# Down-projections of a decoder trunk's third part regrouped into four pairs with a ninth tile apart, and two units per feed-forward block put on ScalarE and VectorE in written order

## The chip, the core and the metric

The kernel runs on one core of a Trainium2 chip. The metric is the device time of one execution in microseconds (us); before the change it is 1767.26 us, the median of three runs (1767.1 to 1767.7). Five engines are named as in the profile: PE (TensorE, matrix products; PEld is its weight load), DVE (VectorE), ACT (ScalarE), POOL (GpSimd) and SP (SyncE, which issues the loads).

## The reference

Two layers, each a feed-forward block (SwiGLU), a token mixer (causal convolution beside differential attention), and a second feed-forward block; all data are float32. The change touches the four feed-forward blocks and one sum of squares.

```python
D_MODEL, SEQ, DEPTH, D_FF = 1024, 512, 2, 2816

def rms_norm(x, g):
    return x * lax.rsqrt(jnp.mean(x * x, axis=-1, keepdims=True) + EPS) * g

def swiglu(h, w_gate, w_up, w_down):
    return (jax.nn.silu(h @ w_gate) * (h @ w_up)) @ w_down

for l in range(DEPTH):
    x = x + 0.5 * swiglu(rms_norm(x, ffn1_norm[l]), ffn1_w_gate[l], ffn1_w_up[l], ffn1_w_down[l])
    x = x + mixer(rms_norm(x, mix_norm[l]))
    x = x + 0.5 * swiglu(rms_norm(x, ffn2_norm[l]), ffn2_w_gate[l], ffn2_w_up[l], ffn2_w_down[l])
```

## The kernel before

**Number format.** PE multiplies in a reduced float32 form. Every operand is therefore split: ACT writes its rounded copy ("hi"), DVE subtracts that from the operand and writes the rest ("lo"), and each product is three matmuls: hi by hi, hi by lo, lo by hi (`product`, L380 to L389). A matmul here has 128 rows of weights and 128 columns; what varies is the width of what streams past, 256 or 512.

**Three parts of a feed-forward block.** The 22 tiles of 128 hidden channels are worked in three parts of 5, 8 and 9 (`PARTS`, L45). The first is computed plainly. The other two are cut into units with Strassen's scheme (seven half-size products in place of eight): a `GateUp` unit (L464) computes gate and up of one hidden tile in 7 products of 4 steps, 84 matmuls of width 256; a `Down` unit (L511, four to a part, q = 0 to 3) computes two output tiles from the part's hidden tiles. A Down unit takes hidden tiles in pairs: p pairs cost 7 products of p steps, 21 p matmuls of width 256; every hidden tile outside the pairs ("plain") costs 6 matmuls of width 512. `PARTS` gives four pairs of eight tiles to the second part, and three pairs and three plain tiles of nine to the third.

**Names in a unit** (`Unit.body`, L399 to L451): a product is named by its weights, such as "u2u1", "u2", "g1", "g2", "all", "g1u2u1"; the seventh, "g1u1", is run inside the next unit (`rest`). Results lie in PSUM halves a, d (first bank) and b, c (second bank). ACT copies some out into `keep` (L405, L422, L442), DVE adds them up (`close`, `rest`).

**Weights.** While a unit runs, the next one's weights are made ready: SP loads them into a ring of five buffers `wraw`, POOL forms the weight sums (L360 to L363), ACT and DVE split four tiles A, B, C (width 1024) and D (width 512) into `whi` and `wlo` (L370, L374; rings of four, and of two for D). In the third part the ninth tile's weights are appended to C and D.

**Hidden tiles.** `Gated` (L633) keeps each hidden tile's hi and lo (`hh`, `hl`), and for a pair the sums "t2", "t3" and "t4" (`hs`, made by `combine`, L691). The unit that follows the last gate of a part and stands before its first Down ("spare" unit) is in the second part the first gate of the third; the third part has none, its ninth gate runs ahead of the second part's Downs.

**Order.** PE's products stand in written order (L389 pins the first matmul of each). Everything else is ordered by a scheduler, on each engine, from the written program. Finished rows of x are normalised for the next block by `Prep.tile` (L229: hi, lo and the square, which POOL adds to `ssum`, L244).

Of the kernel before, what the change touches and what calls it, by code (L numbers as in the profile page):

```python
# [18 lines left out]
P = 128  # L19
# [25 lines left out]
PARTS = ((0, 5, 0), (5, 8, 4), (13, 9, 3))  # L45
# [3 lines left out]
SPACE = 312  # L49
# [21 lines left out]
def trunk(ctx: ExitStack, tc: tile.TileContext, xt, par, lamv, relb, onehot,  # L71
# [110 lines left out]
    ones = const.tile([P, P], F32, tag="ones", name="ones")  # L182
    G.memset(ones, 1.0)
# [37 lines left out]
    class Prep:  # L221
# [16 lines left out]
        def squares(self, k, pin=False):  # L238
            sq = self.s if k == 0 else tmp.tile([P, SEQ], F32, tag="sq", name="sq")
            square = S.activation(sq, x[:, k, :], AF.Square)  # L240
            if pin:
                tc.keep_in_program_order(square)
            if k > 0:
                (V if pin else G).tensor_tensor(self.s, self.s, sq, op=ALU.add)  # L244
# [105 lines left out]
    class Unit:  # L350
# [49 lines left out]
        def body(self, nxt, prev, prev2):  # L400
# [8 lines left out]
            if not self.sums_last:  # L409
                self.go(self.d, "u2", "t4", first=True)  # L410
            self.early()
            if nxt and self.early_free:
                nxt.hi("B")
            if self.sums_last:
                self.go(self.a, "g1", "b11", first=True)
            if prev:
                prev.rest()
            if self.sums_last:
                self.go(self.d, "u2", "t4")
            else:  # L420
                self.go(self.a, "g1", "b11")
# [3 lines left out]
            if nxt and self.early_free:  # L425
                nxt.lo("B")
# [13 lines left out]
            self.go(self.c, "all", "b22")  # L440
            self.go(self.a, "g1u2u1", "t2")
            pinned(S.activation(self.keep[:, 2], self.a, AF.Copy))  # L442
            self.close()
            if nxt:
                nxt.lo("C")
                if not self.early_free:
                    nxt.hi("B")
                    nxt.lo("B")

        early_free, soon, sums_last = True, False, False  # L450
# [13 lines left out]
    class GateUp(Unit):  # L464
        steps = KT // 2

        def __init__(self, fp, halves, g, u, n, gated):
            super().__init__(fp)
            self.halves, self.src, self.n, self.gated = halves, (g, u), n, gated
            self.soon = n == 2 * gated.pairs - 1 and n + 1 == gated.many  # L470
# [33 lines left out]
        def finish(self, n):  # L504
            if self.soon and n == 0:
                self.gated.combine(self.n, self.banks[0], self.banks[1][:, :HS])
            self.gated.add(self.n, self.banks[0], n)

        def combine(self):
            self.gated.combine(self.n, self.banks[0])  # L510

    class Down(Unit):
        def __init__(self, fp, dn, m0, many, pairs, q, h, after, early_free, last):
# [3 lines left out]
            self.early_free = early_free  # L517
            self.sums_last = not q and 2 * pairs == many

        def load(self):  # L520
            A, B = 2 * self.q, 2 * self.q + 1
            whole, over, J = min(self.many, 8), max(self.many - 8, 0), self.steps * P
# [16 lines left out]
            at = {"D": J, "C": 2 * J}  # L539
            raw = {"D": d, "C": more}  # L540
            where = ("D", "D") if J + 2 * over * P <= 512 else ("D", "C")
            self.ninth = []
            for n, m in enumerate((A, B)):
                k = where[n]
                self.ninth.append((k, at[k] // P))
                pull(raw[k], at[k], m, whole, self.many)
                at[k] += over * P
# [9 lines left out]
            cols = {"A": whole * P, "B": whole * P, **at}  # L557
            self.raw = {k: t[:, : cols[k]] for k, t in (("A", u), ("B", g), ("C", more), ("D", d))}

# [7 lines left out]

        def plain(self, ps, n, first=False):
            if 2 * self.steps == self.many:
                return  # L570
            w = [
                self.w("BA"[n], k) if k < 8 else self.w(*self.ninth[n])
                for k in range(2 * self.steps, self.many)
            ]
            self.product(ps, zip(w, (self.h.hh[k] for k in range(2 * self.steps, self.many))), first)

        def spare(self):
            if 2 * self.steps < self.many:
                self.ps = bank(("tp", "y")[self.q % 2], "ps_d")
                self.plain(self.ps, 1, first=True)  # L580

        def early(self):
            if self.early_free and not self.last:
                self.spare()

        def middle(self):
            if self.early_free and not self.last:
                self.plain(self.banks[1], 0)

# [5 lines left out]
        def close(self):  # L595
            A, B = 2 * self.q, 2 * self.q + 1
            two, keep = by_two(self.banks[1]), self.keep
            late = not self.early_free or self.last
            rest = 2 * self.steps < self.many
            if self.last:  # L600
                self.spare()
            elif late:
                self.plain(self.banks[1], 0)
            pinned(V.tensor_tensor(two, two, keep[:, 0::2], op=ALU.add))
            if self.last:
                self.plain(self.banks[1], 0)
            else:
                self.into(A, two, 0.5)
                self.after(A)
            if late and not self.last:  # L610
                self.spare()
            if rest:
                pinned(V.tensor_tensor(by_two(self.ps), by_two(self.ps), keep[:, 1::2], op=ALU.subtract))
                self.into(B, by_two(self.ps), 0.5)
            if self.last:
                self.into(A, two, 0.5)
                self.after(A)

        def rest(self):
            self.go(self.a, "g1u1", "t3")  # L620
            B = 2 * self.q + 1
            if 2 * self.steps < self.many:
# [6 lines left out]

    class Gated:  # L630

        def __init__(self, fp, pairs, many):
            self.fp, self.pairs, self.many = fp, pairs, many  # L633
            self.hold = ("hh7", "hl7") if many > 8 else ("hh8", "hl8")
            self.hh, self.sums, self.held, self.slots = {}, [], {}, []

        def part(self):

            if not self.slots:
# [3 lines left out]
                tags += [(tmp, "ssum", 1), (tmp, "sq", None), (tmp, "sq", None)]  # L643
                self.slots += [
                    lambda pool=pool, tag=tag, bufs=bufs: pool.tile(
                        [P, SEQ], F32R, tag=tag, name="hs", **({"bufs": bufs} if bufs else {}))
                    for pool, tag, bufs in tags
                ]
            return self.slots.pop(0)()

# [10 lines left out]
        def add(self, n, us, step):  # L661
            a, b = slice(0, HS), slice(HS, SEQ)
            first = self.paired(n) and n % 2 == 0
            if step == 0:
                if first:
                    self.held[n] = self.fp.tile([P, SEQ], F32, tag=self.hold[n // 2 % 2], name="hold")
# [12 lines left out]
        def part_hi(self, n, us):  # L679
            hi = self.fp.tile([P, SEQ], F32R, tag=f"hh{n}", name="hh")  # L680
            lo = self.fp.tile([P, SEQ], F32R, tag=f"hl{n}", name="hl")
# [7 lines left out]
        def combine(self, n, us, last=None):  # L689
# [9 lines left out]
            pinned(S.activation(four[:, a], last, AF.Copy))  # L699
            pinned(S.activation(hi, t, AF.Copy))  # L700
            pinned(V.tensor_tensor(four[:, b], last, f32(four[:, a]), op=ALU.subtract))
            pinned(V.tensor_tensor(lo, t, f32(hi), op=ALU.subtract))
            self.sums.append((hi, lo, four))
# [9 lines left out]
    def ffn(pr, gu, dn, after, turn, lead=None, aside=None):  # L713
        with tc.tile_pool(name="ffn", bufs=1) as fp:
# [50 lines left out]
            for m0, many, pairs in PARTS[1:]:  # L765
                h = Gated(fp, pairs, many)
                gates = [
                    GateUp(fp, halves, gu[m0 + n, 0], gu[m0 + n, 1], n, h)
                    for n in (*range(8, many), *range(min(many, 8)))
                ]  # L770
                end = m0 + many == FT
                units += gates[:1] + downs + gates[1:]
                downs = [
                    Down(fp, dn, m0, many, pairs, q, h, after if end else lambda m: None, q > 0 or not end,
                         end and q == KT // 2 - 1)
# [7 lines left out]
            for k in "ABDC":  # L783
                units[0].hi(k, False)
                units[0].lo(k, False)
            for n, unit in enumerate(units):
# [470 lines left out]
```

## Time and profile before

| | value |
|---|---|
| median of three runs | 1767.26 us |
| the profiled execution's own time | 1767.6 us |
| its span (first to last instruction) | 1765.8 us |
| granted TensorE clock, whole span | 1.0 |
| busy: PE / DVE / ACT / POOL | 99% / 79% / 56% / 49% |

The profile describes one execution. A row of the timeline gives start, duration, engine, line, operation, and in square brackets what ended a wait. A row of the groups gives the number of instructions, their total busy time, the mean of one in ns, and the engine's idle time just before them with its releaser. PE's durations overlap: a matmul of width 256 is shown with 0.28 us although the next one starts sooner, so the pace is read from start to start.

### The profile page before, as it was taken

Reading aid. Unit: us, or ns where it says so; the run is one execution under the profiler, and the core shown is the slowest. Engines: PE = TensorE matmul, PEld = TensorE weight load, DVE = VectorE, ACT = ScalarE, POOL = GpSimd, SP = SyncE. Lnnn points to the kernel's source line nnn. Section 1 sums busy time; section 2 is a strip of 40 time slices with the busy share of each in tenths; the row PEclk is TensorE's granted clock in tenths of the full one; section 3 lists DMA queues with packets and bytes.
Section 4 is the critical chain, followed back from the end, with each engine's and each line's share of the span. In section 5 each row is a group of like instructions: output and inputs, shape, how many; then the busy total and the mean of one; then the engine's idle time right before and its main releaser. Section 6 shows DMA issues by size and latency. Waiting matters only on the chain.

```text
span 1765.8 us, 30565 instructions
## 1 busy us (share of the span) xinstructions
PE 1756.3 (99%) x11869; PEld 1620.8 (92%) x11869; DVE 1394.2 (79%) x2021; ACT 989.1 (56%) x1591; POOL 869.5 (49%) x665
## 2 busy tenths in 40 slices
PE   9999999999999999999999999999999999999999
PEld 7899999988788899999988999999887888999998
DVE  6978878868857868878778788777788588788785
ACT  6456565545845456556534665565558354565653
POOL 3165655369753146555303565543687432556551
PEclk9999999999999999999999999999999999999999
DMA  6233333333122233333332333334230232333332
GB/s 226 92 117 100 106 108 105 127 104 99 33 84 84 84 96 108 109 102 117 106 108 72 108 99 105 108 98 154 72 119 25 72 108 72 107 98 108 108 106 75
DMA packets 82930, 177.89 MB, mean 101 GB/s; under 512 B 8951, under 2 KB 30726, under 8 KB 82784
## 3 DMA queue, kind: packets, MB, share of 16 engines
q1 hardware_dynamic: 81184, 174.10, 31.2%
q8 instruction: 93, 1.52, 0.4%
q0 software_dynamic: 1312, 1.67, 0.3%
q14 instruction: 53, 0.43, 0.1%
q10 hardware_dynamic: 288, 0.16, 0.0%
HBM read 173.79 MB, written 3.42 MB: 100 GB/s over the span
## 4 chain that ended last, share of the span: by engine, by line
PE 97%; DVE 2%; DMA 0%; issue 0%; SPq 0%; ACT 0%; DVEq 0%
PE ps_pair L387 57%; PE ps_pair L147 5%; PE ps_pair L146 5%; PE ps_pair L143 5%; PE ps_d L147 2%; PE ps_d L146 2%; PE ps_d L143 2%; PE ps_sc L1028 2%; PE ps_d L387 2%; PE ps_pair L904 2%; PE ps_pair L905 2%; PE ps_pair L906 2%; PE ps_out L146 1%; PE ps_out L147 1%; PE ps_out L143 1%; PE ps_o L1058 1%
## 5 line engine op out<-in xcount | busy, mean ns | idle before, releaser
L374 DVE TENSOR_TENSOR wlo<-wraw,whi 128x1024 fp32r<-128x1024 f32 (+2 forms) x400 | 505.6, 1264 | 167.3 <-ACT whi L370 166.6
L370 ACT ACTIVATE whi<-wraw 128x1024 fp32r<-128x1024 f32 (+2 forms) x400 | 379.2, 949 | 329.4 <-PE ps_pair L387 184.5
L360 POOL TENSOR_TENSOR wraw<-wraw 128x512 f32<-128x512 f32 (+1 forms) x100 | 113.1, 1131 | 605.9 <-DVE wlo L374 393.9
L387 PE MATMUL ps_pair<-acth,wlo 128*128 128x256 f32 x1088 | 307.9, 283 | 0.0
L387 PE MATMUL ps_pair<-actl,whi 128*128 128x256 f32 x1088 | 307.9, 283 | 0.0
L387 PE MATMUL ps_pair<-acth,whi 128*128 128x256 f32 x1088 | 307.9, 283 | 0.0
L387 PE MATMUL ps_pair<-th,whi 128*128 128x256 f32 x816 | 230.9, 283 | 0.0
L387 PE MATMUL ps_pair<-tl,whi 128*128 128x256 f32 x816 | 230.9, 283 | 0.0
L387 PE MATMUL ps_pair<-th,wlo 128*128 128x256 f32 x816 | 230.9, 283 | 0.0
L387 PEld LDWEIGHTS ps_pair<-actl,whi 128*128 128x128 f32 x1088 | 208.9, 192 | 0.2
L387 PEld LDWEIGHTS ps_pair<-acth,whi 128*128 128x128 f32 x1088 | 208.9, 192 | 0.2
L106 ACT ACTIVATE whi<-wraw 128x1024 fp32r<-128x1024 f32 (+3 forms) x124 | 123.2, 1002 | 153.0 <-PE ps_pair L146 85.7
L387 PEld LDWEIGHTS ps_pair<-acth,wlo 128*128 128x128 f32 x1088 | 208.9, 192 | 0.0
L362 POOL TENSOR_TENSOR wraw<-wraw 128x512 f32<-128x512 f32 (+1 forms) x100 | 176.5, 1765 | 7.8
L146 PE MATMUL ps_pair<-actl,whi 128*128 128x512 f32 x448 | 174.7, 391 | 0.3
L143 PE MATMUL ps_pair<-acth,whi 128*128 128x512 f32 x448 | 173.7, 392 | 0.7 <-ACT whi L106 0.6
L147 PE MATMUL ps_pair<-acth,wlo 128*128 128x512 f32 x448 | 173.8, 390 | 0.0
L387 PEld LDWEIGHTS ps_pair<-th,whi 128*128 128x128 f32 x816 | 156.7, 192 | 0.0
L387 PEld LDWEIGHTS ps_pair<-tl,whi 128*128 128x128 f32 x816 | 156.7, 192 | 0.0
L387 PEld LDWEIGHTS ps_pair<-th,wlo 128*128 128x128 f32 x816 | 156.7, 192 | 0.0
L363 POOL TENSOR_TENSOR wraw<-wraw 128x512 f32<-128x512 f32 (+1 forms) x100 | 143.1, 1431 | 7.8
L387 PE MATMUL ps_pair<-hl,whi 128*128 128x256 f32 (+1 forms) x496 | 145.6, 294 | 0.0
(205 smaller groups left out, 4382.5 us busy)
## 6 DMA issues: line engine op xcount, KB each, us to landing
wraw<-in_gu SPq DMA_DIRECT2D x172, 512.0 KB, 3.8
wraw<-in_wqkv SPq DMA_DIRECT2D x24, 512.0 KB, 3.7
wraw<-in_wag SPq DMA_DIRECT2D x16, 512.0 KB, 3.6
wraw<-in_wout SPq DMA_DIRECT2D x16, 512.0 KB, 3.5
wraw<-in_dn SPq DMA_DIRECT2D x60, 128.0 KB, 3.1
wraw<-in_dn SPq DMA_DIRECT2D x20, 384.0 KB, 3.2
wraw<-in_dn SPq DMA_DIRECT2D x28, 256.0 KB, 3.2
wraw<-in_dn SPq DMA_DIRECT2D x20, 320.0 KB, 3.5
```

Of the source, the lines that this page charges most:

```text
L106: S.activation(hi, raw, AF.Copy)
L143: first = T.matmul(ps, wh, xh, start=start, stop=False)
L146: T.matmul(ps, wh, xl, start=False, stop=False)
L147: T.matmul(ps, wl, xh, start=False, stop=stop)
L360: G.tensor_tensor(d, g1, u1, op=ALU.add)
L362: G.tensor_tensor(m0, g1, u1, op=ALU.add)
L363: G.tensor_tensor(m1, g2, m0, op=ALU.add)
L370: pinned(S.activation(hi, raw, AF.Copy), pin)
L374: pinned(V.tensor_tensor(out=lo, in0=raw, in1=f32(hi), op=ALU.subtract), pin)
L387: mm = T.matmul(ps, l, r, start=first and i == n == 0, stop=False, skip_group_check=True)
L904: T.matmul(ps[n], xh[:, t], wh, start=k == 0, stop=False)
L905: T.matmul(ps[n], xh[:, t], wl, start=False, stop=False)
```

## The change

- The third part has four pairs and one plain tile. Its ninth gate unit now runs last, as the spare unit between the eighth gate and the first Down; the second part keeps its spare unit.
- The ninth tile's weights for all eight output tiles are loaded once, in eight pieces, by the first Down into one more `wraw` buffer, and split once into `nine` (`part_ninth`) in the space of the gate units' sums. The first Down runs its six ninth-tile matmuls at its end, the others in their early and middle places.
- Spare unit and first Down of both parts get bodies of their own, and under `tc.manual_schedule` ACT and DVE run them as written. The eighth gate's sums are split in two steps (`fourth` in the spare unit, `settle` in the first Down). In the last Down of a third part the two last products change places, so that "all" ends it, and the plain tiles no longer stand behind it.
- The fourth pair of the third part keeps its sums in `acth[:, 7]`, `actl[:, 7]` and the former `ones_r`; hidden tiles move by one place (`spot`).
- The square of a row tile is written 6 floats into its buffer, and POOL's operands change places.

```diff
-PARTS = ((0, 5, 0), (5, 8, 4), (13, 9, 3))
+PARTS = ((0, 5, 0), (5, 8, 4), (13, 9, 4))
...
-            sq = self.s if k == 0 else tmp.tile([P, SEQ], F32, tag="sq", name="sq")
+            sq = self.s if k == 0 else tmp.tile([P, SEQ + 8], F32, tag="sq", name="sq")[:, GAP : GAP + SEQ]
...
-                (V if pin else G).tensor_tensor(self.s, self.s, sq, op=ALU.add)
+                (V if pin else G).tensor_tensor(self.s, sq, self.s, op=ALU.add)
...
+        def tail(self):
+            return (self.c, "all", "b22"), (self.a, "g1u2u1", "t2")
...
@@ class GateUp @@
+        def body(self, nxt, prev, prev2):
+            if not (prev and prev.soon):
+                return super().body(nxt, prev, prev2)
+            nxt.load()
+            self.begin()
+            self.go(self.c, "u2u1", "t1", first=True)
+            S.activation(self.keep[:, 3], self.c, AF.Copy)
+            nxt.hi("A")
+            nxt.lo("A")
+            self.go(self.d, "u2", "t4", first=True)
+            nxt.hi("B")
+            nxt.lo("B")
+            prev.rest()
+            nxt.hi("D")
+            nxt.lo("D")
+            self.go(self.a, "g1", "b11")
+            S.activation(self.keep[:, :2], by_two(self.banks[0]), AF.Copy)
+            gated, us = prev.gated, prev.banks[0]
+            gated.part_hi(prev.n, us)
+            gated.combine(prev.n, us, prev.banks[1][:, :HS])
+            gated.part_lo(prev.n, us)
+            gated.fourth()
+            self.go(self.b, "g2", "b21")
+            nxt.hi("C")
+            self.go(self.c, "all", "b22")
+            self.go(self.a, "g1u2u1", "t2")
+            S.activation(self.keep[:, 2], self.a, AF.Copy)
...
+            if self.left and not self.q:
+                self.h.ninth = ring("wraw")[:, :1024]
+                for m in range(KT):
+                    pull(self.h.ninth, m * P, m, whole, self.many)
...
@@ class Down @@
+        def body(self, nxt, prev, prev2):
+            if self.q:
+                return super().body(nxt, prev, prev2)
+            if nxt:
+                nxt.load()
+            self.begin()
+            self.go(self.c, "u2u1", "t1", first=True)
+            S.activation(self.keep[:, 3], self.c, AF.Copy)
+            prev.close()
+            self.lo("C")
+            self.h.settle()
+            self.go(self.a, "g1", "b11", first=True)
+            prev.rest()
+            nxt.hi("A")
+            nxt.lo("A")
+            nxt.hi("D")
+            nxt.lo("D")
+            self.go(self.b, "g2", "b21")
+            self.go(self.d, "u2", "t4")
+            S.activation(self.keep[:, :2], by_two(self.banks[0]), AF.Copy)
+            prev.finish(0)
+            prev.finish(1)
+            prev.finish(2)
+            if self.left:
+                self.h.part_ninth()
+            nxt.hi("B")
+            nxt.lo("B")
+            self.go(self.c, "all", "b22")
+            nxt.hi("C")
+            self.go(self.a, "g1u2u1", "t2")
+            S.activation(self.keep[:, 2], self.a, AF.Copy)
+            self.close()
+            nxt.lo("C")
...
+        def tail(self):
+            return super().tail()[:: -1 if self.last else 1]
...
+        def part_ninth(self):
+            th = self.fp.tile([P, 6, SEQ], F32R, tag="th", name="nine")
+            self.nine = hi, lo = [th[:, 2 * n : 2 * n + 2, :].rearrange("p n c -> p (n c)") for n in range(2)]
+            S.activation(hi, self.ninth, AF.Copy)
+            V.tensor_tensor(lo, self.ninth, f32(hi), op=ALU.subtract)
...
+                if prev and prev.soon:
+                    fixed.enter_context(tc.manual_schedule(engines={mybir.EngineType.Activation, mybir.EngineType.DVE}))
+                unit.body(*around(n))
+                if prev2 and prev2.soon:
+                    fixed.close()
```

PE at the end of the third part's first Down, first layer. Before: the last matmuls of "g1u2u1" and then the plain tiles by the first of the two outputs (hh and hl are a hidden tile's hi and lo, whi and wlo the weights'; the second output's nine follow into ps_d):

```order
L387 MATMUL ps_pair_3587<-hs_3540,whi_3533 128x256
L387 MATMUL ps_pair_3587<-hs_3539,wlo_3534 128x256
L387 MATMUL ps_pair_3588<-hh_3512,whi_3481 128x512
L387 MATMUL ps_pair_3588<-hl_3513,whi_3481 128x512
L387 MATMUL ps_pair_3588<-hh_3512,wlo_3482 128x512
L387 MATMUL ps_pair_3588<-hh_3638,whi_3481 128x512
L387 MATMUL ps_pair_3588<-hl_3639,whi_3481 128x512
L387 MATMUL ps_pair_3588<-hh_3638,wlo_3482 128x512
L387 MATMUL ps_pair_3588<-hh_2115,whi2_3517 128x512
L387 MATMUL ps_pair_3588<-hl_2116,whi2_3517 128x512
L387 MATMUL ps_pair_3588<-hh_2115,wlo2_3518 128x512
```

Now, at the same place:

```order
L385 MATMUL ps_pair_3601<-actl_80,whi_3562 128x256
L385 MATMUL ps_pair_3601<-acth_79,wlo_3563 128x256
L385 MATMUL ps_pair_3602<-hh_3682,nine_3686 128x512
L385 MATMUL ps_pair_3602<-hl_3683,nine_3686 128x512
L385 MATMUL ps_pair_3602<-hh_3682,nine_3686 128x512
L385 MATMUL ps_d_3730<-hh_3682,nine_3686 128x512
L385 MATMUL ps_d_3730<-hl_3683,nine_3686 128x512
L385 MATMUL ps_d_3730<-hh_3682,nine_3686 128x512
```

Eighteen matmuls of width 512 have become six, all of the ninth tile; the third of them is the first to use the low part of `nine`.

ACT in the same unit, now, in the order in which it must run (L589, L601 and L612 are the copies into keep, L488 the spare unit's Silu, L769 the eighth gate's sums, L368 the weights' hi, L741 the ninth tile's hh, L707 the hi of `nine`):

```order
L589 ACTIVATE keep<-ps_pair 128x256
L488 ACTIVATE keep<-ps_pair 128x2x256
L769 ACTIVATE acth<-hold 128x512
L368 ACTIVATE whi<-wraw 128x1024
L368 ACTIVATE whi_3653<-wraw_3592 128x512
L601 ACTIVATE keep<-ps_pair 128x512
L741 ACTIVATE hh<-ps_pair 128x512
L707 ACTIVATE nine<-wraw 128x1024
L368 ACTIVATE whi<-wraw 128x1024 x2
L612 ACTIVATE keep<-ps_pair 128x256
```

The hi of `nine` is new, and stands behind L601, which needs the product "u2" of this unit. On DVE the low part of `nine` (L708) stands behind the ninth tile's hl (L746).

DVE at the very end of the program. Before (L604 adds keep into the second bank, L613 into ps_d, L591 adds into x):

```order
L604 TENSOR_TENSOR ps_pair<-ps_pair,keep 128x512
L613 TENSOR_TENSOR ps_d<-ps_d,keep 128x512
L591 SCALAR_TENSOR_TENSOR x<-ps_d,x 128x512
L591 SCALAR_TENSOR_TENSOR x<-ps_pair,x 128x512 x2
L1252 UNCONDITIONAL_BRANCH
```

Now (L647, L653 and L637 are the same three):

```order
L653 TENSOR_TENSOR ps_d<-ps_d,keep 128x512
L637 SCALAR_TENSOR_TENSOR x<-ps_d,x 128x512
L647 TENSOR_TENSOR ps_pair<-ps_pair,keep 128x512
L637 SCALAR_TENSOR_TENSOR x<-ps_pair,x 128x512 x2
L1321 UNCONDITIONAL_BRANCH
```

The addition for the second bank, which before stood first, now comes after the two operations on ps_d.

More of the change, by code (lines that the diff above doesn't have):

```diff
@@ L566, in feats @@
             return self.h.get(xt, j)
[L568 to L575 removed]
+        def body(self, nxt, prev, prev2):
+            if self.q:
+                return super().body(nxt, prev, prev2)
+            if nxt:
+                nxt.load()
[27 more added lines that the diff above has]
+            nxt.lo("C")
```

149 lines of the change are left out of this document (68 added, 81 removed).

## The prediction

> **What bounds the kernel now.** I read the head of the page first, then PE's waits, then PE's timeline.
>
> ```profile
> span 1765.8 us, 30565 instructions
> PE 1756.3 (99%) x11869; PEld 1620.8 (92%) x11869; DVE 1394.2 (79%) x2021; ACT 989.1 (56%) x1591; POOL 869.5 (49%) x665
> PEclk9999999999999999999999999999999999999999
> PE 97%; DVE 2%; DMA 0%; issue 0%; SPq 0%; ACT 0%; DVEq 0%
> ```
>
> PE is busy for 99% of the span at full clock, and the chain that ended last is PE's for 97%. A busy PE need not be a PE at its peak, so the waits come next.
>
> ```profile
> PE ps_o L1058 <- DVE actl L1088: 1.6, 2, 0.8
> ...
> PE ps_sc L1028 <- DVE mn L1032: 0.5, 2, 0.3
> ```
>
> This answer has five lines, the largest 1.6 us, and none names a Gate or Down unit (L387). There PE waits for nobody, and the change can win only through fewer or shorter matmuls, and lose through waits that are new. The pace is read from the first matmul of four units in a row: the last gate of the third part, then Downs 0, 1 and 2.
>
> ```profile
> 290.72 0.28 PE L387 MATMUL ps_pair<-acth,whi 128*128 128x256 f32 x1
> 300.80 0.28 PE L387 MATMUL ps_pair<-hh,whi 128*128 128x256 f32 x1
> 312.82 0.28 PE L387 MATMUL ps_pair<-hh,whi 128*128 128x256 f32 x1
> 324.50 0.28 PE L387 MATMUL ps_pair<-hh,whi 128*128 128x256 f32 x1
> ```
>
> The gate's 84 matmuls of width 256 take 10.08 us: 0.120 us each. Down 1 takes 11.68 us for 63 of width 256 (7.56 us) and 18 of width 512, so 4.12 / 18 = 0.229 us for each of these. One of width 512 costs less than two of width 256.
>
> **The change, part by part.**
>
> *Four pairs in the third part.* Each Down gains one pair (21 matmuls of width 256: 2.52 us) and loses two plain tiles (12 of width 512: 2.75 us). That is 0.23 us less; with four Downs in each of four blocks **-3.6 us**. It is PE's own time and lies on the path.
>
> The Trainium skill, "TensorE: Matmul & The Clock Gate", section "Wait — 56ns, not 53.3ns?", gives a warm matmul its columns at 2.4 GHz plus about 2.5 ns. By it (an estimate) a matmul would take 109 and 216 ns, the gain would be 16 x 296 ns = 4.7 us, and the time 1763.4. The trace does not agree: 120 and 229 ns, so each matmul has a larger fixed part, and 21 narrow ones pay it more often than 12 wide ones.
>
> *The ninth tile in the first Down.* Here a wait may be new. I set the Down's first matmul at 0 and count 1.44 us a product (12 x 0.120): "u2u1" from 0, "g1" 1.44, the spare unit's last product 2.88, "g2" 4.32, "u2" 5.76 (its last matmul starts at 7.08), "all" 7.20, "g1u2u1" 8.64, the ninth tile's six from 10.08. The third of these, at 10.08 + 2 x 0.229 = 10.54, needs the low part of `nine`. How soon an engine follows another is read here:
>
> ```profile
> 1748.87 0.28 PE L387 MATMUL ps_pair<-hs,wlo 128*128 128x256 f32 x1
> 1749.19 0.38 ACT L442 ACTIVATE keep<-ps_pair 128x256 f32<-128x256 f32 x1 [2.06 <-PE ps_pair L387]
> 341.14 0.58 ACT L422 ACTIVATE keep<-ps_pair 128x512 f32<-128x512 f32 x1
> 341.62 0.71 ACT L231 ACTIVATE acth<-x,par 128x512 fp32r<-128x512 f32 x1
> 336.31 1.06 ACT L106 ACTIVATE whi<-wraw 128x1024 fp32r<-128x1024 f32 x1 [1.41 <-issue]
> 337.40 1.23 DVE L107 TENSOR_TENSOR wlo<-wraw,whi 128x1024 fp32r<-128x1024 f32 x1 [0.66 <-ACT whi L106]
> ```
>
> ACT starts 0.32 us after the start of the matmul that it waits for; the next ACT instruction starts 0.48 us after a copy of 512 columns; a hi of width 1024 takes 1.06, DVE follows 0.03 later and takes 1.23 alone. In the written order the keep copy L601 starts at 7.08 + 0.32 = 7.40, hh at 7.88, the hi of `nine` at 8.36, ending 9.42; its low part runs from 9.45 to 10.68. What PE then loses is read where it waited for a weight once:
>
> ```profile
> 8.50 0.52 ACT L106 ACTIVATE whi<-wraw 128x384 fp32r<-128x384 f32 x1 [1.38 <-DMA wraw<-in_gu]
> 9.07 0.50 PE L143 MATMUL ps_pair<-acth,whi 128*128 128x512 f32 x1 [0.57 <-ACT whi L106]
> 9.41 0.40 PE L146 MATMUL ps_pair<-actl,whi 128*128 128x512 f32 x1
> ```
>
> PE starts 0.05 us after the weight's end (8.50 + 0.52 = 9.02), and the next matmul follows 0.34 us later in place of 0.229. So the third matmul stands at 10.73, 0.19 late, and 0.11 more is lost behind it: 0.30 us in each of four first Downs, **+1.2 us**. It lies on the path. What waits behind L601 on ACT is hh, `nine`, the next unit's B and C and a keep copy; of these only `nine` is due within the unit. DVE must be free by 9.45:
>
> ```profile
> L374 DVE TENSOR_TENSOR wlo<-wraw,whi 128x1024 fp32r<-128x1024 f32 x284 | 410.7, 1446 | 154.3 <-ACT whi L370 153.6
> L374 DVE TENSOR_TENSOR wlo<-wraw,whi 128x512 fp32r<-128x512 f32 x100 | 73.6, 736 | 6.0 <-ACT whi L370 6.0
> L687 DVE TENSOR_TENSOR hl<-ps_pair,hh 128x512 fp32r<-128x512 f32 x68 | 46.3, 681 | 2.7 <-ACT hh L682 2.7
> L502 DVE SCALAR_TENSOR_TENSOR ps_pair<-ps_pair,keep 128x512 f32<-128x512 f32 x68 | 47.5, 699 | 2.1
> L500 DVE TENSOR_TENSOR ps_pair<-ps_pair,keep 128x256 f32<-128x256 f32 x68 | 28.8, 424 | 3.0 <-PE ps_pair L387 3.0
> ```
>
> The spare unit's sums start at 4.20 + 0.32 = 4.52 and take 0.42 twice and 0.70, to 6.1; the next unit's A to 7.5 and D to 8.3; the ninth's hl waits for hh (8.47) and ends at 9.2. So it is free. Bounds: 0 if this chain is 0.3 us shorter than I have it; with the mean low part of 1.45 and two whole copies of 0.58 before it, 0.3 + 0.22 + 0.20 = 0.72, 2.9 us in all. I take 1.2, since POOL should be idle then and the operation nearest to it in kind and state took 1.23.
>
> *The squares.* After the mixer PE loses time at one place whose waiting operand comes late from DVE:
>
> ```profile
> 548.06 4.13 DVE L232 SCALAR_TENSOR_TENSOR actl<-x,par,acth 128x512 fp32r<-128x512 f32 x3
> 553.25 0.74 DVE L232 SCALAR_TENSOR_TENSOR actl<-x,par,acth 128x512 fp32r<-128x512 f32 x1
> 548.34 3.30 POOL L244 TENSOR_TENSOR ssum<-ssum,sq 128x512 f32<-128x512 f32 x2 [1.62 <-ACT sq L240]
> 553.51 0.40 PE L143 MATMUL ps_pair<-acth,whi 128*128 128x512 f32 x1
> 554.05 0.50 PE L146 MATMUL ps_pair<-actl,whi 128*128 128x512 f32 x1
> L244 POOL TENSOR_TENSOR ssum<-ssum,sq 128x512 f32<-128x512 f32 x35 | 52.2, 1492 | 89.2 <-ACT sq L240 88.8
> L963 POOL TENSOR_TENSOR csum<-csq,csum 128x512 f32<-128x512 f32 x6 | 6.6, 1093 | 4.6 <-ACT csq L962 3.0 <-ACT csum L959 1.6
> ```
>
> From 553.51 to 554.05 are 0.54 us, 0.31 above the pace: L146 starts 0.06 us after DVE's last L232 ends. Three L232 took 4.13 us beside POOL's additions; one alone takes 0.74. The convolution's sum L963 has the new offset and operand order already and takes 1.09 us in place of 1.49. If the additions of 1.65 become 1.09, DVE loses a third less of its 1.9 us, and the 0.31 us go; if not, nothing goes. I take 0.2 in each of the two layers, **-0.4 us** (0 to -0.6; the second layer runs the same code).
>
> *Costed at nothing.* The end: PE's last product is 1.44 us, and DVE has two operations of 0.69 between the end of "all" and the last one, so the last starts about when it did, 0.32 us behind PE. The fourth pair's sums and the wider C fall on ACT and DVE (busy 56% and 79%) beside PE's work; without that cover see the second rival. The load for Down 2 waits for the buffer of the ninth tile until 10.7, and has over 11 us until that unit. The first Downs' t4 now comes three products later than its sums.
>
> **Sum.** -3.6 + 1.2 - 0.4 = -2.8 us. Against the profiled execution's 1767.6 that is 1764.8; the median of the runs is 0.3 lower, so I forecast **1764.5 us**, with 1763.8 to 1766.6 its own range. A measurement of this kernel can tell about 0.2%, 3.5 us: faster means below 1763.7, slower above 1770.8.
>
> **Rivals.**
>
> 1. *`nine` is in time.* The margin is only 0.3 us. Against it speaks that the copy L601 in front of it hangs on PE itself. Then -3.6 - 0.4: 1763.2 (1763.0 to 1763.6): faster.
>
> 2. *VectorE becomes the bound in the third part's first Downs* (slower). From 4.52 on DVE must do the three sums, A, D, hl, `nine` and B of width 1024 (to 10.68 + 1.45 = 12.1), then four operations of `close` and the first row's actl, then the next unit's C:
>
> ```profile
> L591 DVE SCALAR_TENSOR_TENSOR x<-ps_pair,x 128x512 f32<-128x512 f32 x64 | 43.9, 689 | 3.8 <-PE ps_pair L387 2.4
> L232 DVE SCALAR_TENSOR_TENSOR actl<-x,par,acth 128x512 fp32r<-128x512 f32 x48 | 52.2, 1106 | 5.7 <-ACT acth L231 5.7
> ```
>
> With 0.69 for each of four, 1.11 for actl, about a microsecond of waiting for the copy before it, and 1.45 for C it is done at 18.4. That C is due in Down 1 at "all": 11.45 + 5 x 1.44 + 6 x 0.229 = 20.0. It decides from 1.6 us more lateness; each further microsecond costs 4 us, and 0.2% slower is reached (2.8 + 3.5) / 4 = 1.6 us beyond that: 1768 to 1772. For it: by this list DVE hardly pauses from 4.52 to 18.4. Against it: DVE is alone while POOL waits for Down 2's load.
>
> 3. *Time goes by columns alone*: a narrow matmul at half of 0.229. Then a Down gains 0.34 us, 5.5 in all: 1762.6. The gate's 10.08 us speak against it.
>
> **How the numbers follow.** The forecast 0.63, rival 1 0.23, rival 2 0.12, rival 3 0.02. The range reaches to rival 1 and a little above the forecast's own: 1763.0 to 1767.5, with some 0.14 of rivals 2 and 3 left out and 0.05 of edges. Faster: rival 1 mostly (0.20), rival 3 (0.02) and the forecast's low edge (0.03): 0.25. Slower: the larger part of rival 2, 0.08. Same: 0.67.
>
> **What will show it.** Each step has its place: Down 1 of the third part should take 11.45 us from first to first matmul; in the first Down the third matmul with `nine` should start about 0.19 us late, with DVE's L708 ending just before it; between 548 and 556 the 0.31 us should shrink and L242 take near 1.1 us; nothing else in PE's waits should be new. I am wrong if PE waits in a spare unit, in the second part's first Down, or in Down 1 at "all".

## The result, and the profile after

The changed kernel takes **1757.46 us** (median of four runs, 1756.6 to 1758.4) where the kernel before takes 1767.26: 9.8 us less, a ratio of **0.9943** with a 95% interval of 0.9927 to 0.9958. The forecast was 1764.5, and its range went down to 1763.0: the gain is 3.5 times the one worked out (2.8 us).

First the head of the changed kernel's page, then the first and the fourth of its five rows of PE's waits:

```profile
span 1756.3 us, 30800 instructions
PE 1746.9 (99%) x12013; PEld 1617.0 (92%) x12013; DVE 1411.9 (80%) x2049; ACT 997.4 (57%) x1607; POOL 884.5 (50%) x664
PEclk9999999999999999999999999999999999999999
PE 95%; DVE 2%; ACT 1%; DMA 1%; issue 0%; SPq 0%; ACTq 0%; DVEq 0%
```

```profile
PE ps_o L1127 <- DVE actl L1157: 1.6, 2, 0.8
...
PE ps_sc L1097 <- DVE mn L1101: 0.5, 2, 0.3
```

By these views little is different: PE is busy for 99% at full clock, and no row of its waits names a unit (L385 now). PE runs 144 matmuls more and is done 9.5 us earlier. The exchange of wide matmuls for narrow ones was worked out at 3.6 us of that, so the matmuls themselves must follow each other more quickly. No view counts that; it is read from start to start. In the kernel before, a stretch of 36 matmuls on `acth` and `actl`, and one of 300 on `hh`, `hl` and `hs`, each from its first matmul to the one behind it:

```profile
103.52 0.28 PE L387 MATMUL ps_pair<-acth,whi 128*128 128x256 f32 x1
107.84 0.28 PE L387 MATMUL ps_pair<-th,whi 128*128 128x256 f32 x1
...
184.16 0.28 PE L387 MATMUL ps_pair<-hs,whi 128*128 128x256 f32 x1
220.16 0.28 PE L387 MATMUL ps_pair<-acth,whi 128*128 128x256 f32 x1
```

The same two stretches in the changed kernel:

```profile
104.04 0.29 PE L385 MATMUL ps_pair<-acth,whi 128*128 128x256 f32 x1
108.36 0.28 PE L385 MATMUL ps_pair<-th,whi 128*128 128x256 f32 x1
...
184.12 0.28 PE L385 MATMUL ps_pair<-hh,whi 128*128 128x256 f32 x1
219.36 0.28 PE L385 MATMUL ps_pair<-acth,whi 128*128 128x256 f32 x1
```

With `acth` it is 4.32 / 36 = 120 ns in both. With `hh` and `hs` it was 36.00 / 300 = 120.0 ns and is 35.24 / 300 = **117.5 ns**, in units of the second part that the change does not regroup. The weight loads beside them tell the same, in the view of groups, of before and then of the changed kernel (the last number ahead of the second bar is the mean of one in ns):

```profile
L387 PEld LDWEIGHTS ps_pair<-acth,whi 128*128 128x128 f32 x1088 | 208.9, 192 | 0.2
L387 PEld LDWEIGHTS ps_pair<-th,whi 128*128 128x128 f32 x816 | 156.7, 192 | 0.0
```

```profile
L385 PEld LDWEIGHTS ps_pair<-acth,whi 128*128 128x128 f32 x1120 | 214.5, 192 | 0.1
L385 PEld LDWEIGHTS ps_pair<-th,whi 128*128 128x128 f32 x816 | 153.8, 189 | 0.0
```

To see what all of it comes to, the span is cut at the starts of matmuls, and each interval is put down to the matmul that it follows (count, us; `h` stands for th, tl, hh, hl and hs). The third column is a run from below, the same instructions with their buffers at other distances:

| | before | after | same_place |
|---|---|---|---|
| width 256 on acth, actl | 3648: 437.9 | 3743: 449.3 | 3743: 449.2 |
| width 256 on h | 4799: 575.7 | 5040: **594.5** | 5040: **603.8** |
| width 512 on hh, hl | 768: 174.7 | 480: 109.9 | 480: 108.8 |
| width 512 with nine | - | 96: 23.9 | 96: 23.6 |
| width 512 on acth, actl | 1536: 354.5 | 1536: 354.4 | 1536: 354.7 |
| the mixer's own, and the rest | 1117: 217.8 | 1117: 218.9 | 1117: 219.9 |
| ahead of the first, behind the last start | 5.2 | 5.3 | 5.3 |

At 120 ns the 5040 narrow matmuls on h would take 604.8 us; they take 10.3 less. The mixer's row also holds the clock: the granted clock was 0.51 from 491 to 494 us in the changed kernel, and 0.50 from 493 to 495 and from 1370 to 1372 us in same_place, where the kernel before has 1.00. With one such stretch the row is 1.1 us longer than before, with two it is 2.1.

### The profile page after: what moved, and what is told of

Its sections match the earlier page's. It is cut to its first block, busy times and chain, and to the rows that moved or that the text cites. A ratio compares the mean times of both kernels' runs of the same rounds, so it can differ in the third digit from the quotient of the medians.

```text
span 1756.3 us, 30800 instructions
## 1 busy us (share of the span) xinstructions
PE 1746.9 (99%) x12013; PEld 1617.0 (92%) x12013; DVE 1411.9 (80%) x2049; ACT 997.4 (57%) x1607; POOL 884.5 (50%) x664
## 4 chain that ended last, share of the span: by engine, by line
PE 95%; DVE 2%; ACT 1%; DMA 1%; issue 0%; SPq 0%; ACTq 0%; DVEq 0%
PE ps_pair L385 54%; PE ps_pair L143 6%; PE ps_pair L147 6%; PE ps_pair L146 6%; PE ps_d L143 2%; PE ps_d L147 2%; PE ps_d L146 2%; PE ps_sc L1097 2%; PE ps_out L143 2%; PE ps_out L146 2%; PE ps_out L147 2%; PE ps_pair L975 2%; PE ps_pair L973 2%; PE ps_pair L974 2%; PE ps_o L1127 1%; PE ps_v L1004 1%
## 5 line engine op out<-in xcount | busy, mean ns | idle before, releaser
L372 DVE TENSOR_TENSOR wlo<-wraw,whi 128x1024 fp32r<-128x1024 f32 (+1 forms) x400 | 508.3, 1278 | 136.7 <-ACT whi L368 132.7
L368 ACT ACTIVATE whi<-wraw 128x1024 fp32r<-128x1024 f32 (+1 forms) x400 | 377.5, 952 | 265.3 <-PE ps_pair L385 129.9
L358 POOL TENSOR_TENSOR wraw<-wraw 128x512 f32<-128x512 f32 x100 | 118.4, 1184 | 603.9 <-DVE wlo L372 316.0
L385 PE MATMUL ps_pair<-acth,wlo 128*128 128x256 f32 x1120 | 317.9, 284 | 0.0
L385 PE MATMUL ps_pair<-acth,whi 128*128 128x256 f32 x1120 | 317.4, 283 | 0.0
L385 PE MATMUL ps_pair<-actl,whi 128*128 128x256 f32 x1120 | 317.1, 283 | 0.0
L385 PE MATMUL ps_pair<-th,whi 128*128 128x256 f32 x816 | 229.1, 281 | 0.0
L385 PE MATMUL ps_pair<-tl,whi 128*128 128x256 f32 x816 | 228.0, 279 | 0.0
L385 PE MATMUL ps_pair<-th,wlo 128*128 128x256 f32 x816 | 228.0, 279 | 0.0
L385 PEld LDWEIGHTS ps_pair<-acth,whi 128*128 128x128 f32 x1120 | 214.5, 192 | 0.1
L385 PEld LDWEIGHTS ps_pair<-actl,whi 128*128 128x128 f32 x1120 | 213.9, 191 | 0.2
L385 PEld LDWEIGHTS ps_pair<-acth,wlo 128*128 128x128 f32 x1120 | 214.1, 191 | 0.0
L360 POOL TENSOR_TENSOR wraw<-wraw 128x512 f32<-128x512 f32 x100 | 171.4, 1714 | 7.8
L146 PE MATMUL ps_pair<-actl,whi 128*128 128x512 f32 x448 | 174.7, 391 | 0.0
L385 PEld LDWEIGHTS ps_pair<-th,whi 128*128 128x128 f32 x816 | 153.8, 189 | 0.0
L385 PEld LDWEIGHTS ps_pair<-th,wlo 128*128 128x128 f32 x816 | 153.6, 188 | 0.0
L385 PEld LDWEIGHTS ps_pair<-tl,whi 128*128 128x128 f32 x816 | 153.5, 188 | 0.0
L361 POOL TENSOR_TENSOR wraw<-wraw 128x512 f32<-128x512 f32 x100 | 149.1, 1491 | 7.8
L385 PE MATMUL ps_pair<-hh,whi 128*128 128x256 f32 x512 | 143.4, 280 | 0.0
```

The lines of the kernel that those rows point to most:

```text
L146: T.matmul(ps, wh, xl, start=False, stop=False)
L358: G.tensor_tensor(d, g1, u1, op=ALU.add)
L360: G.tensor_tensor(m0, g1, u1, op=ALU.add)
L361: G.tensor_tensor(m1, g2, m0, op=ALU.add)
L368: pinned(S.activation(hi, raw, AF.Copy), pin)
L372: pinned(V.tensor_tensor(out=lo, in0=raw, in1=f32(hi), op=ALU.subtract), pin)
```

## The experiments

**The theories.** The change gives the two buffers of the squares 8 floats more each. They stand behind the weights' buffers and ahead of those of `th`, `tl`, `hh`, `hl` and most of `hs`, which so move by 64 bytes against the weights; `acth` and `actl` stand ahead of the weights and do not. By the program's allocation `whi` starts at byte 94112 of a partition before and at 93920 after, `acth` at 59296 and 59104, `th` at 163744 and 163616. Modulo 512 that is 416, 416 and 416 before, and 224, 224 and 288 after: `th`, `hh` and `hs` stood at the weights' place and are now 64 bytes from it. Theory A: this distance sets the pace. Theory B, the rival: the new order, the fourth pair and the squares set it. Theory C: a buffer's place counts by itself. In the diffs, `gap0` and `gap1` are unused tiles; they add no instruction, and their numbers are floats (4 bytes) per partition, and `{...}` stands for the line's old text. `SPACE` is room in the buffer of a constant that lies ahead of all of these (the change has 392 there and drops another constant, so `whi` and `acth` move by the same 192 bytes).

**apart64**: the kernel before, with the distance alone.

```diff
-    RING = {"wraw": 5, "whi": 4, "wlo": 4, "wraw2": 1, "whi2": 2, "wlo2": 2}
+    RING = {"wraw": 5, "whi": 4, "wlo": 4, "wraw2": 1, "whi2": 2, "wlo2": 2}; tmp.tile([P, 16], F32, tag="gap1", name="gap1", bufs=1)
```

> The kernel before with one unused tile of 64 bytes per partition placed between the weights' buffers and everything allocated behind them; no instruction is added. In the kernel before the rows of the moving operands th, tl, hh, hl, hs and the rows of whi and wlo start at the same place modulo 512 bytes, and their matmuls of width 256 follow each other in 120 ns; in the changed kernel they start 64 bytes apart, and follow in 118 ns, while acth and actl, still at the weights' place, keep 120. Theory A (the distance of the start addresses sets the pace): about 4,800 matmuls of width 256 go from 120 to 117.8 ns (-10.5 us), about 770 of width 512 that read hh and hl go from 227 to 229 or 231 (+1.8), so 1767.3 - 8.7 = 1758.6 us, 1757 to 1760. Theory B (the shorter time comes from the changed order and the fourth pair, and the pace with it): 1767.3, within 1 us.

Measured: 1761.22 us against 1767.75, ratio 0.9962 (0.9950 to 0.9975). The 300 matmuls on hs, hl and hh in this run:

```profile
183.92 0.28 PE L387 MATMUL ps_pair<-hs,whi 128*128 128x256 f32 x1
219.26 0.28 PE L387 MATMUL ps_pair<-acth,whi 128*128 128x256 f32 x1
```

35.34 us in place of 36.00, and over the program 117.9 ns on h and 120.1 on acth: 565.9 us in place of 575.7, with 1.4 lost on wide hh and hl. This part is as theory A has it. The time is 1.2 us above its range; in the profiled execution the mixer takes 1.6 us more than before, and the granted clock was 0.54 from 1364 to 1367 us there. The one execution of the five with a mean clock of 1.000 took 1759.1 us. Theory B falls: no instruction was changed.

**together**: the changed kernel without the 64 bytes.

```diff
-            sq = self.s if k == 0 else tmp.tile([P, SEQ + 8], F32, tag="sq", name="sq")[:, GAP : GAP + SEQ]
+            sq = self.s if k == 0 else tmp.tile([P, SEQ], F32, tag="sq", name="sq")
```

> The changed kernel with the tile of the squares at its old size, SEQ in place of SEQ + 8, and without its offset: two buffers of 32 bytes less, so everything behind the weights moves back by 64 bytes and stands again at the weights' place modulo 512 bytes. Theory A: th, tl, hh, hl and hs return to 120 ns (some 5,000 matmuls by 2.2 ns, +11.1 us), hh and hl of width 512 to 227 (-1.3): about 1767 us, 1765 to 1768.5. Theory B (order, fourth pair, and squares off POOL's way): the squares were estimated at 0.4 us, so 1757.5 + 0.4 = 1757.9, within 1 us.

Measured: 1766.41 us, ratio 0.9993 (0.9984 to 1.0002). Nearly the whole gain is gone, and the 300 matmuls take 36.00 us again:

```profile
184.03 0.28 PE L385 MATMUL ps_pair<-hh,whi 128*128 128x256 f32 x1
220.03 0.28 PE L385 MATMUL ps_pair<-acth,whi 128*128 128x256 f32 x1
```

**all_moved**: the kernel before, everything behind one constant 64 bytes later.

```diff
-SPACE = 312
+SPACE = 328
```

> The kernel before with SPACE 328 in place of 312: all buffers behind it, weights and moving operands alike, stand 64 bytes later, and their distances from each other stay. Theory A (the distance counts): 1767.3, within 1 us, and 120 ns throughout. Theory C (the place itself counts, not the distance): 1757 to 1760, since hh, th and hs stand 64 bytes later as they do in the first run.

Measured: 1767.75 us, ratio 1.0001 (0.9992 to 1.0010), and 36.00 us for the 300 matmuls. Theory C falls.

**acth_apart**: the changed kernel, with `acth` and `actl` off the weights' place too.

```diff
-    RING = {"wraw": 5, "whi": 4, "wlo": 4, "wraw2": 1, "whi2": 2, "wlo2": 2}
+    RING = {"wraw": 5, "whi": 4, "wlo": 4, "wraw2": 1, "whi2": 2, "wlo2": 2}; wp.tile([P, 16], F32, tag="gap0", name="gap0")
```

> The changed kernel with one unused tile of 64 bytes per partition between actl and the weights' buffers: acth and actl now stand 64 bytes from the weights modulo 512 as well, the other moving operands stay 64 bytes from them. Theory A: about 3,700 matmuls of width 256 that read acth or actl go from 120 to 118 ns (-7 us), about 2,000 of width 512 with them go from 227 to 229 on average, as hh and hl did (+4 to +5): 1757.5 - 2.5 = 1755, 1751 to 1757. Theory B: 1757.5, within 1 us.

Measured: 1751.65 us, ratio to before 0.9909 (0.9896 to 0.9923), 5.8 us less than the changed kernel. Narrow matmuls on acth go from 120.0 to 116.1 ns (-14.9 us), wide ones from about 229 to 235 (+8.2); h stays at 117.9. So the sign or something beside the distance counts: `acth` lies 64 bytes before the weights, `hh` 64 bytes behind them. Both runs point to the weights as the other end of the distance: the new tile of apart64 moves h against all that stands ahead of it, and only h changes its pace; the one here moves `acth` against all that stands behind it, and only `acth` changes in the mean. The weights' buffers alone lie between the two tiles.

**dist32, dist128, dist256, dist448**: the kernel before, with one distance ahead of the weights and the same behind them (the edit of dist32; the others have 32, 64 and 112).

```diff
-SPACE = 312
+SPACE = 56
...
+    RING = {...}; wp.tile([P, 8], F32, tag="gap0", name="gap0"); tmp.tile([P, 8], F32, tag="gap1", name="gap1", bufs=1)
```

> The kernel before with an unused tile of 32 bytes per partition ahead of the weights' buffers and another behind them (SPACE 56 in place of 312 makes the room and moves everything by 1024 bytes together): acth and actl start 32 bytes before the weights modulo 512, th, hh and hs 32 bytes behind them. Two forms of theory A. A1, only the same place is slow: 116 ns for width 256 with acth, 118 with th, hh and hs, as at 64 bytes; wide matmuls 235 and 229 ns; 1767.7 - 6.5 - 5.8 (the two gains measured at 64 bytes) = 1755.4 us, 1753 to 1757.5. A2, the distance counts: paces between those at 0 and at 64 bytes, 1756 to 1766.

> As the run before, with 128 bytes in each of the two tiles: acth and actl 128 bytes before the weights, the others 128 behind. A1: 116, 118, 235 and 229 ns, 1753 to 1757.5 us. A2: other paces than at 64 bytes; if they go on as from 0 to 64 bytes, narrow ones quicker and wide ones slower than there, 1748 to 1762.

> As before, with 256 bytes in each tile: modulo 512 the distance of acth and of th, hh, hs from the weights is the same, 256 bytes. If only the distance counts, the narrow matmuls of both groups have one pace, and so have the wide ones; if the tile or what runs beside it sets the pace, acth keeps a pace 2 ns below that of th and hh. A1: 1753 to 1757.5 us. Were the period 256 bytes or less, 120 and 227 ns and 1767.7 us.

> As before, with 448 bytes in each tile: modulo 512, acth and actl now start 64 bytes behind the weights and th, hh and hs 64 bytes before them, the signs of the first and fourth runs exchanged. If the signed distance counts: th, hh and hs at 116 ns and wide hh at 235 (4,800 x -4 ns = -19 us, 768 x 8 ns = +6), acth at 118 and wide 229 (about -3.5): 1767.7 - 16.5 = 1751 us, 1749 to 1754. If the sign counts for nothing and the tile or its neighbours set the difference: paces as in the first and fourth runs, 1755.4, 1753 to 1757.5.

The mean from start to start, in ns, by the distance of the moving operand from the weights in bytes (intervals under 400 ns; narrow is width 256, wide 512; each ratio is to runs of before on the same chip, 1767.75 to 1768.82 us). By the allocation, up to 320 of the narrow matmuls on h read an `hs` that stands elsewhere:

| run | acth, h | narrow acth | narrow h | wide acth | wide hh | us | ratio to before |
|---|---|---|---|---|---|---|---|
| before | 0, 0 | 120.0 | 120.0 | 229.6 | 227.5 | 1767.26 | |
| apart64 | 0, +64 | 120.1 | 117.9 | 229.4 | 229.3 | 1761.22 | 0.9962 |
| acth_apart | -64, +64 | 116.1 | 117.9 | 235.3 | 228.9 | 1751.65 | 0.9909 |
| dist32 | -32, +32 | 118.1 | 116.8 | 235.1 | 233.2 | 1763.06 | 0.9971 (0.9961 to 0.9982) |
| dist128 | -128, +128 | 119.0 | 119.0 | 234.8 | 232.6 | 1774.40 | 1.0037 (1.0024 to 1.0050) |
| dist256 | -256, +256 | 120.0 | 120.0 | 229.5 | 227.5 | 1768.80 | 1.0001 (0.9992 to 1.0010) |
| dist448 | -448, +448 | 117.4 | 114.9 | 231.8 | 233.1 | 1747.77 | 0.9881 (0.9866 to 0.9896) |

dist256 has the paces and the time of before: the pattern repeats after **256 bytes**, half of what I had compared by. A1 falls: the distance counts, with its sign, and narrow matmuls are quicker and wide ones slower away from 0. A2 has the time of dist32 right, but not its form: at +32 h has 116.8 ns, which is not between 120.0 at 0 and 117.9 at +64. dist448 is -64 for h and +64 for acth, and ends 1.2 us below the range that I gave; h has 114.9 ns there and had 117.9 at +64. In its profile the 300 matmuls take 34.67 us:

```profile
182.62 0.28 PE L387 MATMUL ps_pair<-hs,whi 128*128 128x256 f32 x1
217.29 0.28 PE L387 MATMUL ps_pair<-acth,whi 128*128 128x256 f32 x1
```

dist128 is slower than before, outside what either form allowed: it gains 8.4 us on narrow matmuls and loses 12 on wide ones and 3 on the mixer's.

**same_place**: the whole change at the distance of before (64 bytes of the squares and 192 of the gap are 256).

```diff
-SPACE = 392
+SPACE = 384
...
+    RING = {...}; tmp.tile([P, 48], F32, tag="gap1", name="gap1", bufs=1)
```

> The whole change, with an unused tile of 192 bytes per partition behind the weights' buffers (and SPACE 384 in place of 392, to make room): with the 64 bytes of the squares' wider tiles it makes 256, the distance at which the kernel before keeps its paces of 120 and 227 ns. All instructions are those of the changed kernel. If the addresses were all that the prediction missed, this is the time it should have had: 1764.5 us of the forecast, 0.3 more with the wait for the ninth tile at 0.37 in place of 0.30 us: 1764.8, 1763 to 1766.5. If the changed kernel's instructions bring more than the forecast's 2.8 us, it is below 1763; if the four pairs bring less, above 1766.5 (1766.4 was measured without the squares' offset).

Measured: **1764.58 us**, ratio 0.9983 (0.9975 to 0.9992): what the change brings by its instructions alone (1.4 to 4.4 us by the interval), and what the forecast says, 1764.5. Two terms can be read in it. From the spare's plain tile of Down 1 to that of Down 2, and the second and third matmul with `nine`:

```profile
315.16 0.39 PE L385 MATMUL ps_d<-hh,nine 128*128 128x512 f32 x1
326.62 0.39 PE L385 MATMUL ps_d<-hh,nine 128*128 128x512 f32 x1
```

```profile
310.82 0.40 PE L385 MATMUL ps_pair<-hl,nine 128*128 128x512 f32 x1
311.27 0.50 PE L385 MATMUL ps_pair<-hh,nine 128*128 128x512 f32 x1
```

A Down takes 11.46 us, and the third matmul comes 0.45 us after the second, 0.22 late.

**far_side**: the changed kernel with the distance that was best for narrow matmuls, -64 bytes, for all moving operands but a few `hs`.

```diff
-SPACE = 392
+SPACE = 384
...
+    RING = {...}; wp.tile([P, 16], F32, tag="gap0", name="gap0"); tmp.tile([P, 32], F32, tag="gap1", name="gap1", bufs=1)
```

> The changed kernel with unused tiles of 64 bytes ahead of the weights' buffers and 128 bytes behind them (SPACE 384): acth, actl, th, tl, hh, hl and hs all start 64 bytes before the weights' place modulo 256. Theory A with the measured paces: acth as in the fourth run (116 ns, time 1751.65 us), the others at 115 in place of 117.9 ns (5,040 x 2.9 = -14.6 us), wide matmuls of hh and hl 233 in place of 229 (+2.3): 1739.3 us, 1736 to 1743. Rival: units get 4% shorter, and VectorE (80% busy) or ScalarE can't follow in some of them: new waits of PE in units, above 1743.

Measured: 1741.58 us (1736.5 to 1743.3), ratio 0.9852 (0.9837 to 0.9867). The rival is there as well, though small: PE now waits in units, for a copy (L435) and for `nine`:

```profile
PE ps_pair L385 <- ACT keep L435: 3.2, 5, 1.3
...
PE ps_pair L385 <- DVE nine L708: 0.7, 4, 0.2
```

**far_nine** and **far_swapped**: far_side with the ninth tile's split ahead of the keep copy; and far_side with that split and the one of D exchanged, which is the edit shown (far_nine leaves D where it was, ahead of `part_ninth`).

```diff
-            nxt.hi("D")
-            nxt.lo("D")
+            if self.left:
+                self.h.part_ninth()
             self.go(self.b, "g2", "b21")
...
             prev.finish(2)
-            if self.left:
-                self.h.part_ninth()
+            nxt.hi("D")
+            nxt.lo("D")
```

> The run before with the two instructions that split the ninth tile moved ahead of the keep copy of the first Down, right behind the next unit's D, on ScalarE and VectorE alike. If the wait is set by what stands ahead of these two on ScalarE, PE no longer waits at the third matmul with nine: 0.37 us less in each of four first Downs, -1.5 us against the run before (-0.09%, about what can be told apart), and the rows of the profile show the matmuls with nine at their pace. If the copy and the sums that now stand behind them come too late, a new wait takes its place at the product all, and the time is the same or up to 2 us more.

> The run far_side with the split of the ninth tile and that of the next unit's D exchanged in the first Down, on ScalarE and VectorE alike. In far_nine VectorE ran A, D, nine and then hl of the last hh without a pause, and PE waited 0.48 us at its second matmul with nine, for hl; in far_side it waited 0.34 us at the third, for nine. If VectorE's queue before that point is the cause, taking D (0.6 to 1.2 us) out of it makes nine and hl ready at about 832.0 and 832.7 us where PE needs them at 832.7 and 832.9: the four waits fall from 0.34 or 0.48 to under 0.1 us each, and the time is 1 to 2 us below far_side and far_nine in the profile (too little for the interval to tell). If the load of the ninth tile or PE's own product is the cause, the waits stay at 0.3 us or more.

Measured: 1737.40 us, ratio 0.9827 (0.9811 to 0.9844), and 1737.41, ratio 0.9833 (0.9819 to 0.9846); neither can be told from far_side by its time. PE's waits, of far_nine and then of far_swapped:

```profile
PE ps_pair L385 <- ACT keep L435: 3.1, 4, 0.9
...
PE ps_pair L385 <- DVE hl L746: 1.0, 3, 0.4
```

```profile
PE ps_pair L385 <- ACT keep L435: 2.8, 5, 1.0
PE ps_o L1127 <- DVE actl L1157: 1.7, 2, 0.8
```

In far_nine my expectation failed: in three of the four first Downs the wait did not go, it moved from `nine` to `hl`, the row behind it on VectorE, and grew from 0.34 to about 0.5 us. With D taken out of the queue in far_swapped no matmul with `nine` comes late any more. So at this pace, once ScalarE's part is early, VectorE's queue is what the ninth tile waits for. In the changed kernel it is not: there VectorE is idle for 0.25 us until ScalarE has written the hi of `nine` (the row of L708 below), as the forecast had it. Both are the quickest of the versions tried, some 20 us below the changed kernel.

## Why the prediction was wrong

**The step that failed** is the first one: "There PE waits for nobody, and the change can win only through fewer or shorter matmuls", with the pace "0.120 us each" taken from the gate of before and kept for every narrow matmul after the change. The sentence names shorter matmuls, and the sum then has none. Its term for them should have been 5040 matmuls by 1.85 ns: 594.5 us in place of 603.8 (same_place), -9.3 us, and +1.1 on wide hh and hl; the medians of the two runs lie 7.1 us apart. A second step hid it: of the squares' new buffer I counted what it does to VectorE, and not that a wider tile moves all tiles behind it. The diff shows it (`SEQ + 8`). The rivals missed it too; all took the paces of before but one, and that one divides by columns.

**The part that the sum did contain was right in the main**, as same_place shows: 1764.58 us against 1764.5. With the terms as measured below it is -3.5 (16 x 0.22) + 1.3 (4 x 0.33) - 0.9 = -3.1 us; the run is 3.3 us below before on its chip (1767.87). That it meets the forecast to 0.1 us is luck: the interval is 3 us wide, and the squares were off by 0.5.

- *Four pairs*: a Down of 11.45 us was forecast; 11.46 in same_place, and 11.28 at the changed kernel's own pace, from Down 1 to Down 2:

```profile
311.11 0.28 PE L385 MATMUL ps_pair<-hh,whi 128*128 128x256 f32 x1
322.39 0.28 PE L385 MATMUL ps_pair<-hh,whi 128*128 128x256 f32 x1
```

  At the old distance the gain is 11.68 - 11.46 = 0.22 us a Down, as the rows had it. By the rule of the Trainium skill ("TensorE: Matmul & The Clock Gate", section "Wait — 56ns, not 53.3ns?") the prediction's estimate was 0.296 us; the trace does not agree.
- *The ninth tile*: the wait is where it was forecast. VectorE's L708, then the second, third and fourth matmul with `nine`:

```profile
308.79 1.23 DVE L708 TENSOR_TENSOR nine<-wraw,nine 128x1024 fp32r<-128x1024 f32 x1 [0.25 <-ACT nine L707]
```

```profile
309.58 0.40 PE L385 MATMUL ps_pair<-hl,nine 128*128 128x512 f32 x1
310.07 0.50 PE L385 MATMUL ps_pair<-hh,nine 128*128 128x512 f32 x1
310.41 0.40 PE L385 MATMUL ps_d<-hh,nine 128*128 128x512 f32 x1
```

  The third starts 0.05 us after L708's end (308.79 + 1.23), 0.26 late, and 0.11 more go behind it: 0.37 in place of 0.30, since PE itself comes earlier; 0.33 in same_place. PE's waits have no row for it: it is the weight load that waits (PEld, four times).
- *The squares*: the stall after the mixer is gone, but not for the reason given. I expected POOL's additions to fall to 1.1 us and the three L232 to shrink. POOL's additions in the changed kernel, then VectorE's operations there, with the first one as it was before in the last fence:

```profile
L242 POOL TENSOR_TENSOR ssum<-sq,ssum 128x512 f32<-128x512 f32 x35 | 53.4, 1524 | 69.3 <-ACT sq L238 68.6
```

```profile
540.41 1.21 DVE L107 TENSOR_TENSOR wlo<-wraw,whi 128x1024 fp32r<-128x1024 f32 x1
...
545.42 4.25 DVE L230 SCALAR_TENSOR_TENSOR actl<-x,par,acth 128x512 fp32r<-128x512 f32 x3
```

```profile
541.68 2.18 DVE L107 TENSOR_TENSOR wlo<-wraw,whi 128x1024 fp32r<-128x1024 f32 x1
```

  The mean addition takes 1.52 us (1.49 before), and the three L230 4.25 (4.13). What became shorter are VectorE's operations ahead of them, so it is done before PE asks. PE gets back 0.46 us in each layer, the losses on both sides of the 0.31 with it: -0.9 in place of -0.4, outside the bound. It stays in the time: the 192 wide matmuls of the output projection do take 46.3 us in same_place and 45.4 in together, but the 0.9 us between them lie in the stretches of same_place with a clock of 0.50; in the second layer of the changed kernel, at full clock, 96 of them take 22.5 us, and 22.6 in together. The offset with its wider tile does it and not the order of the operands: together has the new order alone, and the old stall.
- *The second rival*, VectorE as the bound: no such wait in the changed kernel; when PE was made quicker, its queue did decide in the first Downs (far_nine).

What stays open: why the distance sets the pace. The runs show that it does, its period, and that the place itself does not. It isn't the only thing, either: `acth` at -64 has 116.1 ns in acth_apart, and 114.2 in far_side, where h was moved as well.

## What to carry to other kernels

Where PE never waits, measure its pace from start to start for each kind of operand before and after, since the pages of the profile show 99% busy in both cases. A diff that changes the size of a tile moves every buffer behind it: compare start addresses, not instructions alone, and when an unexplained gain appears, take the addresses back with an unused tile before looking for its cause in the order. With spare bytes left, try the distance between weights and moving operands on purpose: here it was worth more than all regrouping.

## What the runs showed of the hardware

- Matmuls of width 256 in fp32r follow each other in 114 (far_side) to 120 ns (before), and those of 512 in 227 (before) to 235 (acth_apart), by the distance between the start of the moving operand and that of the weights modulo 256 bytes; narrow ones are slowest at distance 0 and wide ones are quickest there.
- With all operands at distance 0, 8,366 of 8,447 narrow intervals are exactly 120 ns; in the changed kernel nearly all lie from 113 to 127, those on `acth`, which is still at 0, with them, though their mean stays at 120.
- A subtraction of width 1024 on VectorE took 2.18 us beside POOL's additions and 1.21 once the squares stood 24 bytes into their (wider) buffer; the next one took 1.98 and 1.78, and POOL's own additions stayed at 1.5 us.
- The granted clock can fall to half for some 3 us inside the mixer: 0.51 from 491 to 494 us in the changed kernel, 1.00 there in the kernel before.
